# The last down projection of a hybrid encoder block: its sixth feature tile in one pass, and the final norm of the first 256 tokens moved behind it

## The chip, the cores and the metric

The kernel runs on one core of a Trainium2 chip. The metric is the device time of one execution in microseconds (us). TensorE (PE) multiplies, with its weight loads shown apart (PEld); VectorE (DVE), ScalarE (ACT) and GpSimd (POOL) do the elementwise work; SyncE (SP) issues most of the loads and stores, which 16 DMA engines carry out.

## The reference, cut to what matters

The block has three token mixers, a gated merge, and a feed-forward part with a convolution. The change touches only the end of the feed-forward part and the final norm. For 512 tokens, 1024 features and 2816 hidden units:

```
def conv_glu_ffn(h, w_up, w_conv, b_conv, w_down):
    a, u = jnp.split(h @ w_up, 2, axis=-1)
    return (jax.nn.gelu(dwconv3(a, w_conv, b_conv)) * u) @ w_down
...
x = x + conv_glu_ffn(rms_norm(x, ffn_norm_g[l]), ...)
return rms_norm(x, final_norm_g)

def rms_norm(x, g):
    y = x * lax.rsqrt(jnp.mean(x * x, axis=-1, keepdims=True) + EPS)
    return y * g
```

All is float32. Each token's final scale needs the sum of its squares over all 1024 features, so over all eight feature tiles of 128.

## The kernel before

**Products.** Every float32 operand is split into a high and a low part, and each product of tiles is three matmuls into the same accumulator: high x high, high x low, low x high. The helper `mm3` records them, so that nearly all matmuls have the lines L213, L214 and L215. A sum over the 11 tiles of a half of the hidden units (k = 0 to 10) is 33 matmuls.

**The down projection.** The hidden units are done in two halves. In each half the product with `w_down` is made feature tile by feature tile: the weights stand still, the hidden activations of 512 tokens move, and the result has features on partitions and tokens along the row. It is added to the residual stream `x2[f]`, a 128 x 512 tile for each f from 0 to 7, four of them in one buffer. In the last half, tiles 0 to 4 take this way (loop at L1379 to L1393): after each, ScalarE squares the finished tile, GpSimd adds the squares to `acc3` (128 x 512), and ScalarE multiplies the tile by the gain of the final norm.

**The last tiles.** `last_tiles` (L1221) does the rest, in an order that lets the ends of the work overlap:

1. Tiles 5, 6 and 7, the first 256 tokens only (`half_tile`: 33 matmuls of 256 columns, then L1237 adds to the residual, L1239 squares, L1240 adds the squares to `acc3`, L1241 multiplies by the gain). Now `acc3` is complete for the first 256 tokens; `two_parts` (L301, L302) splits it into high and low.
2. Tile 5, the other 256 tokens, again 33 matmuls. Behind its k=5 and k=7 stand the two matmuls of `sum_a` (L1251), which sum `acc3` over the partitions. `rstd_wide` (L337 to L341: two operations on ScalarE, three on VectorE) makes the scale of each token out of that.
3. `out_a(0)` multiplies tiles 0 to 3 of the first 256 tokens by that scale (L1257, four operations on VectorE) and stores them (L1260, to outa, 512 KB).
4. Two blocks of 128 tokens (t=2: tokens 256 to 383; t=3: tokens 384 to 511) finish tiles 6 and 7. Here the activations stand still and the weights of both tiles move (256 columns), so that tokens lie on partitions; again 33 matmuls each. In block t=2, behind k=4, `sums` (L1292, L1294) takes the sums of squares of `acc3` for the tokens of both blocks, GpSimd's power (L1218) and L1311 put one of them where block t=3 will read it, and `out_a(4)` scales and stores tiles 4 to 7 of the first 256 tokens. At the end of block t=2, L1334 evicts it, L1336 squares it, L1337 and a GpSimd power make the scale of its tokens, L1340 puts that on a diagonal, L1342 scales the block and L1343 stores it (outc, 128 KB).
5. In block t=3, behind k=7, `row_b` spreads the scale of tokens 256 to 383 over the partitions with a matmul (L1271), scales tiles 0 to 5 of these tokens (L1274, two operations on VectorE) and stores them (L1276, outc, 384 KB). Then tiles 0 to 5 of the last 128 tokens are transposed (L1288), the sum of squares is finished (L1322), a GpSimd power makes the scale, and the two halves of the last block are stored, one from SP (L1327) and one from ScalarE's queue (L1332), to outb, 256 KB each.

A scheduling layer fixes each engine's order of instructions when the program is built. It follows the source, but may put an operation behind a later one that it takes to be ready sooner. Each engine then works through its list in order, and so does each queue of stores.

Of the kernel before, what the change touches and what calls it, by code (L numbers as in the profile page):

```python
# [18 lines left out]
S = 512  # L19
D = 1024  # L20
KT = D // P
# [5 lines left out]
LF = KT - 2  # L27
# [83 lines left out]
def hybrid_block(ctx, tc, xg, xT, memT, wflat, vecs, gbias, nabias, outa, outb, outc):  # L111
# [14 lines left out]
    def nm(s):  # L126
        uid[0] += 1
        return f"{s}_{uid[0]}"
# [4 lines left out]
    def scr(n=512):  # L133
        return sp.tile([P, S], F32, tag="scr", name=nm("s"))[:, :n]

    def tiny(n):
        return tp.tile([P, 32], F32, tag="tiny", name=nm("y"), bufs=12)[:, :n]

    def mmps():
        return mmp.tile([P, 512], F32, tag="mm", name=nm("mm"))  # L140
# [71 lines left out]
    def mm3(ps, lh, ll, rh, rl, start, stop):  # L212
        PE.matmul(ps, lh, rh, start=start, stop=False)  # L213
        PE.matmul(ps, lh, rl, start=False, stop=False)  # L214
        st["mm"] = PE.matmul(ps, ll, rh, start=False, stop=stop).ins  # L215
# [179 lines left out]
    def proj(key, XHs, XLs, n=S, at={}, ps=None):  # L395

        ws = weights(key)
        k0 = 0 if ps is None else 1
        if ps is None:
            ps = mmps()  # L400
        for k in range(k0, KT):
            mm3(ps[:, :n], ws[k][0], ws[k][1], XHs[k], XLs[k], k == 0, k == KT - 1)
            if k in (1, 3, 5):
                flush()
            if k in at:
                at[k]()
        return ps
# [67 lines left out]
    for f in range(4):  # L475
        ps = ps_k[f] if f < 2 else proj(("mlk", f), XH, XL)
# [27 lines left out]
    for c in range(3):  # L504
        n, nk = TMC[c], TMK[c]
        pss = [(mmps if c % 2 else atps)() for _ in range(NT)]
        for h in range(KT // nk):
            ws = weights(("tm", c, h))
            for t in range(NT):
                tsl = slice(t * P, (t + 1) * P)  # L510
                for k in range(nk):
                    kk = nk * h + k
                    ps = pss[t][:, :n]
                    mm3(ps, XH[kk][:, tsl], XL[kk][:, tsl], ws[k][0], ws[k][1], kk == 0, kk == KT - 1)
        for t in range(NT):
            ps = pss[t]
# [562 lines left out]
    def paced(key):  # L1079
        return proj(key, XH, XL, at={k: lambda: step(RB / 4) for k in (1, 3, 5)})  # L1080

    xq = unit()
    for f in range(4):
        ps = proj(("xaq", f), XH, XL)
# [3 lines left out]
    for f in range(4):  # L1088
        ps = paced(("o", f))
# [15 lines left out]
    for f in range(4):  # L1105
        ps = proj(("memk", f), MH, ML, M)
# [15 lines left out]
    for f in range(4):  # L1122
        ps = paced(("naq", f))
# [3 lines left out]
    for f in range(4):  # L1127
        ps = paced(("nak", f))
# [12 lines left out]
    for br in range(3):  # L1141
# [19 lines left out]
        for fp in range(4):  # L1161
# [9 lines left out]
            for i in range(2):  # L1171
                f = 2 * fp + i
                ps = mmps()
# [22 lines left out]
    for f in range(KT):  # L1196
        xr = scr()
        SY.dma_start(xr, xT[f])
        ps = proj(("out", f), GH, GL)
# [4 lines left out]
        else:  # L1204
            sq = scr()
# [7 lines left out]
    Hf = S // 2  # L1213
    half = {}

    def power(v):
        col = tiny(v.shape[-1])
        G.tensor_tensor(col, v, nhalf[:, :v.shape[-1]], op=ALU.pow)  # L1218
        return col

    def last_tiles(U, UL_):  # L1221

        ws = [w for i in range(3) for w in weights(("dnl", i))]
        w5 = weights(("dn", 1, LF - 1, 0)) + weights(("dn", 1, LF - 1, 1))

        def half_tile(f, cs, at={}):
            ps = mmps()[:, :Hf]
            fs = slice((f - LF) * P, (f - LF + 1) * P) if f >= LF else slice(0, P)  # L1230
            for k in range(HF):
                w = ws[k] if f >= LF else w5[k]
                mm3(ps, w[0][:, fs], w[1][:, fs], U[k][:, cs], UL_[k][:, cs], k == 0, k == HF - 1)
                if k in at:
                    at[k]()
            xf = x2[f][:, cs]
            V.tensor_tensor(xf, ps, xf, op=ALU.add)  # L1237
            sq = scr(Hf)
            A.activation(sq, xf, AF.Square)  # L1239
            V.scalar_tensor_tensor(acc3[:, cs], acc3[:, cs], EPS * D / P if f == KT - 1 else 0.0, sq, op0=ALU.add, op1=ALU.add)  # L1240
            A.activation(xf, xf, AF.Copy, scale=vcol("fin_g", f))  # L1241

        for f in range(LF - 1, KT):
            half_tile(f, slice(0, Hf))

        parts = two_parts(acc3[:, :Hf], Hf)

        def sum_a(i):
            if i == 0:
                half["s"] = atps()  # L1250
            PE.matmul(half["s"][:, :Hf], onesr, parts[i], start=i == 0, stop=i == 1)  # L1251
            if i == 1:
                half["r"] = rstd_wide(half["s"], Hf, None)

        def scale_a(eng, *tiles):
            for i in tiles:
                eng.tensor_tensor(x2[i][:, :Hf], x2[i][:, :Hf], half["r"], op=ALU.mult)  # L1257

        def store_a(i):
            SY.dma_start(outa[i * P:(i + 4) * P, :].rearrange("(f p) s -> p f s", p=P), x2v[i // 4][:, :, :Hf])  # L1260

        half_tile(LF - 1, slice(Hf, S), {5: lambda: sum_a(0), 7: lambda: sum_a(1)})
        def out_a(i):
            scale_a(V, *range(i, i + 4))
            store_a(i)

        out_a(0)
        def row_b():

            pb = atps()  # L1270
            PE.matmul(pb[:, :P], ones, half["e"], start=True, stop=True)  # L1271
            o, tsl = half["o"], slice(2 * P, 3 * P)
            for u, n in ((0, 4), (1, LF - 4)):
                V.tensor_tensor(o[:, u * S:u * S + n * P].rearrange("p (f s) -> p f s", f=n), x2v[u][:, :n, tsl],  # L1274
                                pb[:, :P].unsqueeze(1).to_broadcast([P, n, P]), op=ALU.mult)
            SY.dma_start(outc[:, :LF * P], o[:, :LF * P])  # L1276

        banks = [mmps(), mmps()]
        for t in range(2, NT):
            tsl = slice(t * P, (t + 1) * P)  # L1280
            last = t == NT - 1
            bank = banks[t - 2]
            ps = bank[:, :256]
            pts = [atps() if last else None, mmps()]
            r = scr(256)

            def turn(i):
                PE.transpose(pts[i // 4][:, i % 4 * P:(i % 4 + 1) * P], x2[i][:, tsl], ident)  # L1288

            def sums(sl):  # L1290
                pc = atps()
                PE.matmul(pc[:, :1], acc3[:, sl], ones[:, 0:1], start=True, stop=True)  # L1292
                v0 = tiny(1)
                V.tensor_scalar(v0, pc[:, :1], 1.0 / D, EPS, op0=ALU.mult, op1=ALU.add)  # L1294
                return v0

            for k in range(HF):
                mm3(ps, U[k][:, tsl], UL_[k][:, tsl], ws[k][0], ws[k][1], k == 0, k == HF - 1)
                if k == 1 and last:

                    for i in range(LF, KT):
                        PE.matmul(ps[:, (i - LF) * P:(i - LF + 1) * P], x2[i][:, tsl], ident, start=False, stop=False)
                elif k == 1:
                    for i in range(LF, KT):
                        turn(i)
                    A.activation(r, pts[1][:, 256:], AF.Copy)
                if not last and k == 4:
                    v0 = sums(tsl)

                    v1 = sums(slice(S - P, S))  # L1310
                    V.scalar_tensor_tensor(banks[1][:, 256:257], v1, D ** 0.5, power(v1), op0=ALU.mult, op1=ALU.mult)  # L1311
                    out_a(4)
                if last and k == 7:
                    row_b()
            if last:
                for i in range(LF):
                    turn(i)
            sq, v = scr(257), tiny(1)
            if last:
                oa, ob = scr(), scr()  # L1320

                A.activation(sq, bank[:, :257], AF.Square, scale=D ** -0.5, accum_out=v)  # L1322
                A.activation(oa[:, 256:], pts[0][:, 256:], AF.Copy)
                col = power(v)
                A.activation(oa[:, :256], pts[0][:, :256], AF.Copy, scale=col)
                first = V.tensor_scalar(oa[:, 256:], oa[:, 256:], col, None, op0=ALU.mult).ins
                SY.dma_start(outb[:, :512], oa)  # L1327

                with tc.issue_after(first):
                    V.scalar_tensor_tensor(ob[:, 256:], ps, col, gfin, op0=ALU.mult, op1=ALU.mult)  # L1330
                A.activation(ob[:, :256], pts[1][:, :256], AF.Copy, scale=col)
                A.dma_start(outb[:, 512:], ob)  # L1332
                continue
            V.tensor_tensor(r, ps, r, op=ALU.add)  # L1334
            ss = tiny(1)
            A.activation(sq[:, :256], r, AF.Square, accum_out=ss)  # L1336
            V.tensor_scalar(v, ss, 1.0 / D, v0, op0=ALU.mult, op1=ALU.add)  # L1337
            col = power(v)
            half["e"] = scr(P)
            V.tensor_scalar(half["e"], ident, col, None, op0=ALU.mult)  # L1340
            half["o"] = o = unit()
            V.scalar_tensor_tensor(o[:, LF * P:D], r, col, gfin, op0=ALU.mult, op1=ALU.mult)  # L1342
            SY.dma_start(outc[:, LF * P:], o[:, LF * P:D])  # L1343

    for hh in range(2):
# [3 lines left out]
        for j in range(HF):  # L1349
            f = HF * hh + j  # L1350
            if f == 0:
# [8 lines left out]
                k = KT - 1  # L1360
# [8 lines left out]
            sq = scr()  # L1369
# [9 lines left out]
        for f in range(KT if hh == 0 else LF - 1):  # L1379
            ws = weights(("dn", hh, f, 0)) + weights(("dn", hh, f, 1))  # L1380
            ps = mmps()
# [3 lines left out]
            if hh == 1:  # L1385
# [3 lines left out]
                else:  # L1389
                    sq = scr()  # L1390
# [119 lines left out]
```

## Time and profile before

| | us |
|---|---|
| median of 3 runs | 875.1 (875.02 to 875.71) |
| the profiled execution | 874.76 |
| its span in the profile | 873.0 |
| TensorE busy | 867.6 |
| VectorE busy | 593.4 |
| ScalarE busy | 470.7 |
| GpSimd busy | 125.0 |

The granted TensorE clock was 0.999 of full speed. The span runs from the first to the last event of the program; the rest of the device time lies around it. Times in the views are counted from the start of the span. Line numbers with an L are lines of the kernel that was profiled. A row of the timeline gives start, duration, engine, line, operation, output<-input, and in brackets how long the engine had been idle and what released it. "PE 128*128" is the stationary operand, the next size what moves.

### The profile page before, as it was taken

Reading aid. Unit: us, or ns where it says so; the run is one execution under the profiler, and the core shown is the slowest. Engines: PE = TensorE matmul, PEld = TensorE weight load, DVE = VectorE, ACT = ScalarE, POOL = GpSimd, SP = SyncE. Lnnn points to the kernel's source line nnn. Section 1 sums busy time; section 2 is a strip of 40 time slices with the busy share of each in tenths; the row PEclk is TensorE's granted clock in tenths of the full one; section 3 lists DMA queues with packets and bytes.
Section 4 is the critical chain, followed back from the end, with each engine's and each line's share of the span. In section 5 each row is a group of like instructions: output and inputs, shape, how many; then the busy total and the mean of one; then the engine's idle time right before and its main releaser. Section 6 shows DMA issues by size and latency. Waiting matters only on the chain.

```text
span 873.0 us, 12227 instructions
## 1 busy us (share of the span) xinstructions
PE 867.6 (99%) x4303; PEld 735.9 (84%) x4303; DVE 593.4 (68%) x1240; ACT 470.7 (54%) x996; POOL 125.0 (14%) x201
## 2 busy tenths in 40 slices
PE   9999999999999999999999999999999999999997
PEld 7898889888888888888888888888888888888887
DVE  7794789886577768897676558776633466666534
ACT  7563567765455658898544455444422344444532
POOL 0101100000163370600000002111100011111010
PEclk9999999999999999999999999999999999999999
DMA  8324634522253453633233432332233332322412
GB/s 281 100 79 153 204 122 124 169 82 99 83 143 74 118 151 109 158 121 121 98 97 109 145 108 97 97 97 96 76 100 105 107 98 97 98 96 90 136 40 97
DMA packets 39421, 99.81 MB, mean 114 GB/s; under 512 B 5688, under 2 KB 13880, under 8 KB 39360
## 3 DMA queue, kind: packets, MB, share of 16 engines
q1 hardware_dynamic: 31568, 92.32, 33.3%
q0 software_dynamic: 7360, 6.32, 3.5%
q8 instruction: 34, 0.56, 0.3%
q10 hardware_dynamic: 432, 0.39, 0.1%
q14 instruction: 27, 0.22, 0.1%
HBM read 94.80 MB, written 4.21 MB: 113 GB/s over the span
## 4 chain that ended last, share of the span: by engine, by line
PE 98%; DVE 1%; issue 0%; ACT 0%; POOL 0%; POOLq 0%
PE mm L213 29%; PE mm L214 29%; PE mm L215 29%; PE at L214 2%; PE at L213 2%; PE at L215 2%; PE at L938 1%; PE at L761 1%; PE at L919 1%; PE at L900 0%; PE at L901 0%; PE at L748 0%; PE at L1026 0%; PE at L243 0%; PE mm L422 0%
## 5 line engine op out<-in xcount | busy, mean ns | idle before, releaser
L213 PE MATMUL mm<-u,wh 128*128 128x512 f32 (+1 forms) x1072 | 415.0, 387 | 0.0
L215 PE MATMUL mm<-u,wl 128*128 128x512 f32 (+1 forms) x1072 | 411.8, 384 | 0.0
L214 PE MATMUL mm<-u,wh 128*128 128x512 f32 (+1 forms) x1072 | 411.6, 384 | 0.0
L195 ACT ACTIVATE wh<-wr 128x512 fp32r<-128x512 f32 (+2 forms) x298 | 183.7, 621 | 207.1 <-PE mm L214 163.7
L196 DVE TENSOR_TENSOR wl<-wr,wh 128x512 fp32r<-128x512 f32 (+3 forms) x300 | 203.6, 681 | 89.8 <-ACT wh L195 86.7
L215 PEld LDWEIGHTS mm<-u,wl 128*128 128x128 f32 x1072 | 201.4, 188 | 40.2 <-DVE wl L196 0.2
L213 PEld LDWEIGHTS mm<-u,wh 128*128 128x128 f32 x1072 | 201.5, 188 | 38.6 <-ACT wh L195 0.2
L214 PEld LDWEIGHTS mm<-u,wh 128*128 128x128 f32 x1072 | 201.6, 188 | 38.2
L1374 POOL TENSOR_TENSOR s<-s,rb 128x512 f32<-128x512 f32 x22 | 38.2, 1735 | 402.6 <-DVE s L1373 238.9
L542 POOL DMA_DIRECT2D u<-nav_d x128 | 62.3, 511 | 67.2 <-PE at L938 22.7
L219 ACT ACTIVATE u<-s 128x512 fp32r<-128x512 f32 x26 | 16.4, 632 | 57.9 <-DVE s L1377 56.2
L1377 DVE TENSOR_TENSOR s<-mm,s 128x512 f32<-128x512 f32 x22 | 15.2, 690 | 23.8 <-POOL s L1374 23.8
L462 ACT ACTIVATE s<-pad,vec 128x512 f32<-128x512 f32 x30 | 24.4, 813 | 9.7 <-DVE pad L460 9.7
L220 DVE SCALAR_TENSOR_TENSOR u<-s,u 128x512 fp32r<-128x512 f32 x26 | 19.0, 732 | 14.8 <-ACT u L219 14.7
L463 DVE SCALAR_TENSOR_TENSOR s<-pad,vec,s 128x512 f32<-128x512 f32 x30 | 22.5, 750 | 5.5 <-ACT s L462 5.5
L1373 DVE SCALAR_TENSOR_TENSOR s<-s,s 128x512 f32<-128x512 f32 x22 | 15.2, 691 | 13.4 <-ACT s L1372 13.3
L464 DVE SCALAR_TENSOR_TENSOR s<-pad,vec,s 128x512 f32<-128x512 f32 x30 | 22.5, 750 | 0.8
L1372 ACT ACTIVATE s<-s 128x512 f32<-128x512 f32 x22 | 13.9, 632 | 14.9 <-DVE s L1371 14.9
L460 DVE TENSOR_TENSOR pad<-mm,rb 128x512 f32<-128x512 f32 x22 | 15.1, 690 | 6.5 <-PE mm L215 6.4
L1384 DVE TENSOR_TENSOR u<-mm,u 128x512 f32<-128x512 f32 x13 | 9.0, 691 | 14.6 <-PE mm L215 14.6
L213 PE MATMUL mm<-wh,u 128*128 128x512 f32 x48 | 18.8, 392 | 0.0
L214 PE MATMUL mm<-wl,u 128*128 128x512 f32 x48 | 18.7, 390 | 0.0
(341 smaller groups left out, 1051.5 us busy)
## 6 DMA issues: line engine op xcount, KB each, us to landing
wr<-wflat SPq DMA_DIRECT2D x141, 512.0 KB, 3.4
nab<-nabias SPq DMA_DIRECT2D x16, 256.0 KB, 2.7
u<-nav_d POOLq DMA_DIRECT2D x128, 32.0 KB, 2.8
s<-xT SPq DMA_DIRECT2D x15, 256.0 KB, 4.0
wr<-wflat SPq DMA_DIRECT2D x14, 192.0 KB, 2.4
nav_d<-nv POOLq DMA_DIRECT2D x8, 256.0 KB, 3.7
R<-rd SPq DMA_DIRECT2D x8, 256.0 KB, 5.4
wr<-wflat SPq DMA_DIRECT2D x2, 544.0 KB, 3.4
```

Of the source, the lines that this page charges most:

```text
L195: A.activation(h[:, u:v], src, AF.Copy)
L196: V.tensor_tensor(l[:, u:v], src, h[:, u:v].bitcast(F32), op=ALU.subtract)
L213: PE.matmul(ps, lh, rh, start=start, stop=False)
L214: PE.matmul(ps, lh, rl, start=False, stop=False)
L215: st["mm"] = PE.matmul(ps, ll, rh, start=False, stop=stop).ins
L219: A.activation(h, src, AF.Copy, scale=scale)
L220: V.scalar_tensor_tensor(l, src, scale, h.bitcast(F32), op0=ALU.mult, op1=ALU.subtract)
L462: A.activation(t1, pad[:, 0:512], AF.Identity, scale=vcol(w, i), bias=vcol(b, i))
L463: V.scalar_tensor_tensor(t1, pad[:, 1:513], vcol(w, n + i), t1, op0=ALU.mult, op1=ALU.add)
L464: V.scalar_tensor_tensor(t1, pad[:, 2:514], vcol(w, 2 * n + i), t1, op0=ALU.mult, op1=ALU.add)
L542: G.dma_start(vw[r * 32:(r + 1) * 32, i * 256:(i + 1) * 256], nav_v[hf, r, CW[b]:CW[b] + 32, hp * 256:(hp + 1) * 256])
L1374: G.tensor_tensor(c, c, rb2, op=ALU.mult)
```

## The change

Tile 5 of the last half is multiplied in one pass over all 512 tokens ahead of tiles 6 and 7, in place of two passes over 256. With the second pass gone, what stood beside it moves into the blocks: the matmuls of `sum_a` behind k=5 and k=7 of block t=2, `out_a(0)` behind k=7 of block t=2, and `out_a(4)` from k=4 of block t=2 to k=2 of block t=3. The token sums (`sums`) move from k=4 to k=2 of block t=2.

```diff
-        def half_tile(f, cs, at={}):
-            ps = mmps()[:, :Hf]
+        def part_tile(f, cs):
+            n = cs.stop - cs.start
+            ps = mmps()[:, :n]
...
-                if k in at:
-                    at[k]()
...
-            sq = scr(Hf)
+            sq = scr(n)
...
-        for f in range(LF - 1, KT):
-            half_tile(f, slice(0, Hf))
+        part_tile(LF - 1, slice(0, S))
+        for f in range(LF, KT):
+            part_tile(f, slice(0, Hf))
...
-        half_tile(LF - 1, slice(Hf, S), {5: lambda: sum_a(0), 7: lambda: sum_a(1)})
         def out_a(i):
             scale_a(V, *range(i, i + 4))
             store_a(i)
 
-        out_a(0)
...
-                if not last and k == 4:
+                if not last and k == 2:
                     v0 = sums(tsl)
...
+                if not last and k in (5, 7):
+                    sum_a(k // 6)
+                if not last and k == 7:
+                    out_a(0)
+                if last and k == 2:
                     out_a(4)
```

In the built program this gives the following orders. On VectorE, behind tile 7: the two operations of `sums` (L1292 after the change), the write for block t=3 (L1309), then L302, L339, the eviction of block t=2 (L1337), L340, L341, the four scalings of `out_a(0)`, the tiny operation of the scale of tokens 256 to 383 (L1340), one scaling of `out_a(4)`, the diagonal (L1343), L1345, the other three scalings, and the two operations of `row_b` (L1272). On TensorE, the matmul of `row_b` (L1269) stands two matmuls later than before, in k=8 of block t=3. On SP, the store of block t=2 (L1346) goes ahead of the second outa store, and the large outc store (L1274) and the first outb store (L1330) behind it.

## The prediction

> **What bounds the kernel now.** I read the page first, then busy time by stage, then the last 31 us engine by engine, and last the DMA.
>
> ```profile
> span 873.0 us, 12227 instructions
> PE 867.6 (99%) x4303; PEld 735.9 (84%) x4303; DVE 593.4 (68%) x1240; ACT 470.7 (54%) x996; POOL 125.0 (14%) x201
> PE 98%; DVE 1%; issue 0%; ACT 0%; POOL 0%; POOLq 0%
> ```
>
> TensorE is busy through the whole span and carries 98% of the chain that ended last. So a gain or a loss is either TensorE time, or time behind the last matmul, where stores end the span. The change touches only the last 31 us. Next, busy time by stage (length; busy time of PE, PEld, DVE, ACT, POOL; granted clock; DMA share; GB/s). The stages are feature tile 4 at 512 tokens, the first half of tile 5, the halves of tiles 6 and 7, the second half of tile 5 with two row-sum matmuls in it, block t=2, block t=3.
>
> ```profile
> 834.82:842.29 7.47, 7.47 (x34) 6.19 (x33) 2.63 (x4) 2.93 (x5) 1.29 (x1) 1.00 0.15 59
> 842.29:846.25 3.96, 3.96 (x35) 3.95 (x33) 0.69 (x1) 1.36 (x2) 1.29 (x1) 1.00 0.00 0
> 846.25:854.02 7.77, 7.77 (x69) 7.77 (x67) 1.70 (x4) 1.86 (x4) 0.00 (x0) 1.00 0.01 2
> 854.02:858.26 4.24, 4.24 (x37) 4.24 (x36) 1.29 (x4) 2.15 (x5) 0.00 (x0) 1.00 0.00 0
> 858.26:862.92 4.66, 4.66 (x41) 4.62 (x40) 4.16 (x15) 1.13 (x3) 0.69 (x1) 1.00 0.11 34
> 862.92:867.51 4.59, 4.59 (x41) 4.59 (x40) 2.74 (x8) 0.51 (x2) 0.56 (x1) 1.00 0.68 226
> ```
>
> TensorE has no gap and runs at full clock, so these lengths are its prices. VectorE is nearly full in block t=2 (4.16 of 4.66 us) and loosely filled before it (1.29 of 4.24). The stores of the first 256 tokens are most of the DMA share of block t=3. TensorE's marks in the tail:
>
> ```profile
> 857.06 0.28 PE L1251 MATMUL at<-s,onesr 128*128 128x256 f32 x1
> 860.28 0.58 PE L1292 MATMUL at<-ones,acc 128*128 128x1 f32 x4
> 861.75 0.28 PE L215 MATMUL mm<-u,u 128*128 128x256 f32 x1
> 866.23 0.38 PE L1271 MATMUL at<-s,ones 128*128 128x128 f32 x2
> 867.39 0.28 PE L215 MATMUL mm<-u,u 128*128 128x256 f32 x1
> ```
>
> The row at 861.75 is the last matmul of k=7 in block t=2, the one at 867.39 the last of the 33 of block t=3. The other engines in the same stretch:
>
> ```profile
> 857.38 0.38 ACT L337 ACTIVATE s<-at 128x256 f32<-128x256 f32 x1 [1.31 <-PE at L1251]
> 858.25 0.43 DVE L339 SCALAR_TENSOR_TENSOR s<-at,s 128x256 f32<-128x256 f32 x1 [1.72 <-ACT s L338]
> 859.37 0.43 DVE L341 SCALAR_TENSOR_TENSOR s<-s,s 128x256 f32<-128x256 f32 x1
> 860.05 1.42 DVE L1257 TENSOR_TENSOR u<-u,s 128x256 f32<-128x256 f32 x4
> 861.39 0.21 DVE L1294 TENSOR_SCALAR y<-at 128x1 f32<-128x1 f32 x2
> 861.68 0.69 POOL L1218 TENSOR_TENSOR y<-y,nhalf 128x1 f32<-128x1 f32 x1 [16.39 <-DVE y L1294]
> 862.40 0.17 DVE L1311 SCALAR_TENSOR_TENSOR mm<-y,y 128x1 f32<-128x1 f32 x1 [0.47 <-POOL y L1218]
> 862.48 1.09 DVE L1257 TENSOR_TENSOR u<-u,s 128x256 f32<-128x256 f32 x3
> 864.48 0.21 DVE L1337 TENSOR_SCALAR y<-y,y 128x1 f32<-128x1 f32 x1 [0.58 <-ACT s L1336]
> 864.77 0.56 POOL L1218 TENSOR_TENSOR y<-y,nhalf 128x1 f32<-128x1 f32 x1 [2.40 <-DVE y L1337]
> 865.36 0.29 DVE L1340 TENSOR_SCALAR s<-ident,y 128x128 f32<-128x128 f32 x1 [0.67 <-POOL y L1218]
> 865.57 0.48 DVE L1342 SCALAR_TENSOR_TENSOR u<-s,y,gbf 128x256 f32<-128x256 f32 x1
> 867.71 0.39 ACT L1322 ACTIVATE s<-mm 128x257 f32<-128x257 f32 x1 [3.27 <-PE mm L215]
> ```
>
> Then the stores: when the queues issue them, and the DMA while they move.
>
> ```profile
> 861.54 2.49 SPq L1260 DMA_DIRECT2D outa<-u  x2
> 866.07 0.34 SPq L1343 DMA_DIRECT2D outc<-u  x1
> 867.69 0.34 SPq L1276 DMA_DIRECT2D outc<-u  x1
> 869.35 0.33 SPq L1327 DMA_DIRECT2D outb<-s  x1
> 869.72 0.35 ACTq L1332 DMA_DIRECT2D outb<-s  x1
> ```
>
> ```profile
> 862.25:862.50 0.25, 0.25 (x5) 0.25 (x4) 0.10 (x2) 0.00 (x0) 0.12 (x1) 1.00 0.09 29
> 862.25:864.25 2.00, 2.00 (x20) 2.00 (x19) 1.50 (x5) 0.32 (x1) 0.12 (x1) 1.00 0.77 256
> 868.50:869.75 1.25, 0.00 (x0) 0.00 (x0) 0.74 (x2) 0.87 (x3) 0.31 (x1) 1.00 0.81 315
> 870.00:871.75 1.75, 0.00 (x0) 0.00 (x0) 0.00 (x0) 0.00 (x0) 0.00 (x0) 0.64 0.81 300
> 871.50:871.75 0.25, 0.00 (x0) 0.00 (x0) 0.00 (x0) 0.00 (x0) 0.00 (x0) 0.50 0.27 90
> ```
>
> Share times length is the time for which all 16 DMA engines are full: 0.77 x 2.00 = 1.54 us for the first outa store, 0.81 x 1.25 = 1.01 us for the large outc store, 0.81 x 1.75 = 1.42 us for the two outb stores together. Today these three groups do not meet. The last data move until 871.50 + 0.27 x 0.25 = 871.57, and the span ends 873.0 - 871.57 = 1.43 us later.
>
> **TensorE's part.** Tile 5 is now one pass of 33 matmuls over 512 tokens. Tile 4 shows its price, 7.47 us; removed are two passes of 3.96. The second pass lasted 4.24, and the 0.28 above 3.96 are the two row-sum matmuls, which only move. The saving is 2 x 3.96 - 7.47 = 0.45 us. Per matmul that is 0.226 us at 512 tokens and 0.120 at 256.
>
> The Trainium skill (TensorE: Matmul & The Clock Gate, Back-to-back issue gap) gives a warm gap of 262 cycles at 256 columns and 518 at 512, at 2.4 GHz 0.109 and 0.216 us, by which the pass would save only 66 x 0.109 - 33 x 0.216 = 0.07 us and everything below would come 0.38 us later. The trace differs in both gaps, and I keep its rows.
>
> Block t=2 therefore begins at 842.29 + 7.47 + 7.77 = 857.53 (now 858.26). It takes 4.66 + 0.28 = 4.94 us, since the row-sum matmuls lie in it, and block t=3 begins at 862.47 (now 862.92).
>
> **The norm of the first 256 tokens.** The built order puts the second row-sum matmul behind k=7, which is 861.75 + 0.12 - 858.26 = 3.61 us into the block, plus 0.16 for the first one: 861.30. It needs the low part, L302, which VectorE now runs behind L1292 and L1309 (L1294 and L1311 before), so behind a GpSimd power. The token sums move from k=4 to k=2, six matmuls or 0.72 us earlier in the block: 857.53 + 2.02 - 0.72 = 858.83, and end 0.58 later at 859.41. From L1294 to L1311 it takes 862.40 - 861.39 = 1.01, to the next VectorE operation 0.08 more; L302 (0.43, as L339) ends at about 860.93. TensorE does not wait, with 0.37 us to spare.
>
> From the second row-sum matmul ScalarE's first operation is 857.38 - 857.06 = 0.32 us away, L339 1.19 us: 862.49. Now the eviction of block t=2 stands between L339 and L340, where an eviction stood before too, so L341 follows 859.37 - 858.25 = 1.12 us later, at 863.61, and the first scaling at 864.04, when L341 ends. Four scalings take VectorE 861.39 - 860.05 = 1.34 us. Here the order costs something: the tiny operation that starts the norm of tokens 256 to 383 (L1340 after, L1337 before) is queued behind them and runs at 865.38 instead of 864.48, 0.90 us later, though its input is there by then. Behind it, a fifth scaling runs beside the GpSimd power, which I price at the 0.69 us of the row beside wide VectorE work and not at 0.56. So the scaled identity comes 0.90 + 0.13 later, at 866.39, ends at 866.68, and L1345 (L1342 before) starts at 866.60.
>
> TensorE wants that scaled identity (L1269) in k=8 of block t=3, two matmuls later than now: 862.47 + (866.23 - 862.92) + 0.24 = 866.02. It waits 0.66 us there, with all later matmuls and the transposes behind it. The last matmul is then 866.68 + (867.39 - 866.23) - 0.24 = 867.60 (now 867.39), and the tail of block t=3 starts 0.21 us later: the 0.45 is gone.
>
> **The stores.** L1345 holds VectorE for about 0.40 us before the next operation starts (its rows overlap by some 0.08), then three scalings take 1.09: 867.00 + 1.09 = 868.09. The second outa store follows 0.07 later (861.54 against 860.05 + 1.42), at 868.16. Before, both outa stores were issued by 864.03 (861.54 + 2.49). On SP's queue the large outc store and the first outb store come behind it, and none waits long to be issued: the large outc store needs two VectorE operations more, the outb stores come at about 869.6 and 869.9. The data of an outa store start 862.50 - 0.09 x 0.25 - 861.54 = 0.94 us after the issue, so at 869.10. From there the 16 engines have 1.54 + 1.01 + 1.42 = 3.97 us of work without a gap, because each following store is issued before the one ahead has drained. Data end at 873.07, the span 1.43 later at 874.50, against 873.0: +1.50 us. The 0.45 us is inside this number; the tail that it meets is 1.95 us worse.
>
> The bounds of the terms: the GpSimd power at 0.56 takes 0.13 off; the outc store's 384 KB in 1.01 us is 389 GB/s, and the whole backlog (512 + 384 + 512 KB) at that rate takes 3.70, 0.27 off; the outa store's own rate (512 KB in 1.54, 340 GB/s) for all of it takes 4.24, 0.27 on.
>
> The Trainium skill (DMA: Bandwidth & Descriptors, Where 436 GB/s comes from) puts the ceiling at 435 GB/s, by which the backlog would take an estimated 3.31 us and the end would come 0.66 us sooner. The stores of this trace stay below that rate.
>
> The profiled execution is 874.76 us for a span of 873.0, and 0.34 below the median of 875.1. Added to that median: **876.6 us**. This kernel's runs tell about 0.2%, 1.75 us, from no change.
>
> **Rivals.** First, *the stores stay hidden*: SP issues the second outa store so early, or the engines drain so fast, that the last outb store ends the span as now. Then only the 0.21 us of TensorE's late end is left: 875.3; if the scaled identity also came in time, 874.65. For it speaks that the engines stand idle for 0.6 us ahead of the outb data now (868.50 + 1.01 = 869.51 to 871.57 - 1.42 = 870.15), against it that the issue of the second outa store hangs on VectorE's order, which is built in. It would need that store to be issued by 873.0 + 0.21 - 1.43 - 3.97 - 0.94 = 866.87.
>
> Second, *one DMA engine lags*. The two outa stores landed differently:
>
> ```profile
> DMA to landing us min/median/max: 3.0/3.3/3.7
> ```
>
> A store lands when its slowest engine is done, and one took 0.7 us longer than its twin. Now such a lag is hidden in block t=3. With an outa store at the head of the last backlog a late engine carries its delay through to the last outb store: 876.6 + 0.7 = 877.3, slower beyond the bound from a lag of 0.25 us. Against it: with the backlog, other engines' idle time does not help, but the lag may as well have come from the second store queuing behind the first, which the backlog already contains.
>
> Third, *the saving shows*: 875.1 - 0.45 = 874.65, if neither VectorE's order nor the stores cost anything. It is 0.05%, so even this is no change by the bound.
>
> **How the numbers follow.** The forecast, a store backlog that ends between 875.8 and 877.1 by the bounds above, gets 0.68. The hidden stores (with the saving) get 0.11, the lagging engine 0.19, anything better by over 0.2%, which no row supports, 0.02. 876.85 is the bound to slower: the upper sixth of the forecast, about 0.12, lies above it. So slower 0.31, within 0.2% 0.67, faster 0.02. The range 875.3 to 877.3 reaches down to the hidden stores and up to the lagging engine.
>
> **What would show it.** Tile 5 as 33 matmuls in about 7.5 us, and block t=3 starting 0.4 to 0.5 us earlier. The tiny operation L1340 starting right behind four scalings, and TensorE waiting 0.5 to 0.8 us at L1269. The second outa store issued at about 868.2, and the DMA share full without a gap from about 869 to 873. I am wrong if the DMA has a gap there, if the second outa store is issued before 867, or if TensorE waits at the second row-sum matmul instead.

## The result, and the profile after

| | before | after |
|---|---|---|
| median of 22 runs, us | 875.18 (874.66 to 875.89) | 876.63 (876.09 to 877.21) |
| ratio | | 1.0016, 95% interval 1.0009 to 1.0023 |
| span of the profiled execution, us | 873.0 | 875.4 |

The change costs 1.45 us (by the interval 0.8 to 2.0). It is slower beyond the noise of 22 runs, and smaller than the 0.2% that the prediction took as its bound.

The two spans differ by more, and part of that is not the change. In the profiled execution of the changed kernel the first matmul of tile 5 starts at 843.34, and not at 842.29, though nothing ahead of it was changed in the source. The profiles of e1 to e7 below show the same kind of shift, with starts from 842.67 to 843.39. So I count times from the start of tile 5. A page rounds the span to 0.1 us; to two digits the traces have 872.95 before and 875.44 now. The span ends 872.95 - 842.29 = 30.66 us after the start of tile 5 before the change, and 875.44 - 843.34 = 32.10 after it now, which is 1.44 us more and agrees with the runs.

The page of the changed kernel, and busy time by stage (tile 5; tiles 6 and 7; block t=2; block t=3):

```profile
span 875.4 us, 12160 instructions
PE 868.3 (99%) x4270; PEld 735.4 (84%) x4270; DVE 593.9 (68%) x1238; ACT 470.5 (54%) x994; POOL 124.9 (14%) x201
```

```profile
843.34:850.82 7.48, 7.48 (x35) 6.20 (x33) 0.69 (x1) 1.35 (x2) 1.29 (x1) 1.00 0.01 2
850.82:858.59 7.77, 7.77 (x67) 7.77 (x66) 2.23 (x4) 2.29 (x4) 0.00 (x0) 1.00 0.00 0
858.59:863.40 4.81, 4.81 (x43) 4.81 (x42) 1.66 (x6) 2.40 (x6) 0.57 (x1) 1.00 0.00 0
863.40:868.87 5.47, 4.86 (x41) 4.65 (x40) 4.89 (x15) 0.54 (x3) 0.67 (x1) 1.00 0.27 90
```

Tile 5 takes 7.48 us in one pass, against 3.96 twice. Block t=3 starts 863.40 - 843.34 = 20.06 us after tile 5, against 862.92 - 842.29 = 20.63: 0.57 us saved up to there. VectorE's full stretch has moved from block t=2 (now 1.66 of 4.81 us) to block t=3 (4.89 of 5.47), and block t=3 has a hole of 5.47 - 4.86 = 0.61 us on TensorE. The timeline shows what stands around the hole:

```profile
862.21 0.28 PE L1251 MATMUL at<-s,onesr 128*128 128x256 f32 x1
867.72 0.49 PE L1269 MATMUL at<-s,ones 128*128 128x128 f32 x2 [0.61 <-DVE s L1343]
868.75 0.28 PE L215 MATMUL mm<-u,u 128*128 128x256 f32 x1
```

```profile
865.04 1.43 DVE L1257 TENSOR_TENSOR u<-u,s 128x256 f32<-128x256 f32 x4
866.39 0.21 DVE L1340 TENSOR_SCALAR y<-y,y 128x1 f32<-128x1 f32 x1
866.51 0.41 DVE L1257 TENSOR_TENSOR u<-u,s 128x256 f32<-128x256 f32 x1
866.67 0.67 POOL L1218 TENSOR_TENSOR y<-y,nhalf 128x1 f32<-128x1 f32 x1 [5.45 <-DVE y L1340]
867.38 0.29 DVE L1343 TENSOR_SCALAR s<-ident,y 128x128 f32<-128x128 f32 x1 [0.45 <-POOL y L1218]
867.98 1.09 DVE L1257 TENSOR_TENSOR u<-u,s 128x256 f32<-128x256 f32 x3
```

The tiny operation L1340 starts right behind the four scalings, the GpSimd power runs beside a fifth, and the diagonal L1343 is what TensorE waits for at L1269. The last three scalings hold back the second outa store. The queues, the landing times in the list of DMA issues (KB, median us to landing), and the DMA share in the last stretch:

```profile
866.54 0.39 SPq L1260 DMA_DIRECT2D outa<-u  x1
868.09 0.34 SPq L1346 DMA_DIRECT2D outc<-u  x1
869.14 0.38 SPq L1260 DMA_DIRECT2D outa<-u  x1
870.02 0.33 SPq L1274 DMA_DIRECT2D outc<-u  x1
870.71 0.36 SPq L1330 DMA_DIRECT2D outb<-s  x1
871.08 0.35 ACTq L1335 DMA_DIRECT2D outb<-s  x1
```

```profile
outb<-s SPq DMA_DIRECT2D x1, 256.0 KB, 3.5
outb<-s ACTq DMA_DIRECT2D x1, 256.0 KB, 3.4
```

```profile
870.00:874.25 4.25, 0.00 (x0) 0.00 (x0) 0.75 (x2) 0.84 (x2) 0.17 (x1) 0.92 0.94 339
874.00:874.25 0.25, 0.00 (x0) 0.00 (x0) 0.00 (x0) 0.00 (x0) 0.00 (x0) 0.50 0.06 17
```

From 870.0 on the engines are full for 0.94 x 4.25 = 4.00 us without a gap. The last matmul starts at 868.75, and the span ends 6.65 us later. An outb store lands 3.4 to 3.5 us after its issue. Before the change, with the engines idle ahead of the outb data, the same two stores took 2.0 and 2.3:

```profile
outb<-s SPq DMA_DIRECT2D x1, 256.0 KB, 2.0
outb<-s ACTq DMA_DIRECT2D x1, 256.0 KB, 2.3
```

### The profile page after: what moved, and what is told of

Its sections match the earlier page's. It is cut to its first block, busy times and chain, and to the rows that moved or that the text cites. A ratio compares the mean times of both kernels' runs of the same rounds, so it can differ in the third digit from the quotient of the medians.

```text
span 875.4 us, 12160 instructions
## 1 busy us (share of the span) xinstructions
PE 868.3 (99%) x4270; PEld 735.4 (84%) x4270; DVE 593.9 (68%) x1238; ACT 470.5 (54%) x994; POOL 124.9 (14%) x201
## 4 chain that ended last, share of the span: by engine, by line
PE 98%; DVE 0%; issue 0%; ACT 0%; POOL 0%; POOLq 0%; ACTq 0%
PE mm L213 29%; PE mm L215 29%; PE mm L214 29%; PE at L214 2%; PE at L215 2%; PE at L213 2%; PE at L938 1%; PE at L761 1%; PE at L919 1%; PE at L900 0%; PE at L901 0%; PE at L748 0%; PE at L1026 0%; PE at L243 0%; PE mm L422 0%
## 5 line engine op out<-in xcount | busy, mean ns | idle before, releaser
L215 PEld LDWEIGHTS mm<-u,wl 128*128 128x128 f32 x1061 | 199.4, 188 | 40.5
L462 ACT ACTIVATE s<-pad,vec 128x512 f32<-128x512 f32 x30 | 24.4, 813 | 9.7 <-DVE pad L460 9.7
L213 PE MATMUL mm<-wh,u 128*128 128x512 f32 x48 | 18.8, 393 | 0.0
L215 PE MATMUL mm<-wh,u 128*128 128x512 f32 x48 | 18.7, 390 | 0.0
```

The lines of the kernel that those rows point to most:

```text
L462: A.activation(t1, pad[:, 0:512], AF.Identity, scale=vcol(w, i), bias=vcol(b, i))
```

## The experiments

Theory A is the prediction's: the second outa store is issued late and leads a backlog that ends the span; TensorE's wait has no part in that sum, and the merged pass does save its time. Theory B says that TensorE's wait and its late last matmul end the span. Theory C says that the merged pass saves nothing where it stands. The changed kernel and the kernel before it have 22 runs each; each experiment has 11, beside 33 (e1 to e4) or 27 (e5 to e7) of the kernel before on the same chip. "From tile 5" is the end of the span counted from the first matmul of tile 5 (both from the trace, in the column before it), less the 30.66 us of before.

| | median, us | before, us | ratio (95%) | span less start of tile 5, us | from tile 5, us |
|---|---|---|---|---|---|
| changed kernel | 876.63 | 875.18 | 1.0016 (1.0009 to 1.0023) | 875.44 - 843.34 | +1.44 |
| e1 early store | 875.82 | 875.34 | 1.0006 (0.9997 to 1.0015) | 874.05 - 843.06 | +0.33 |
| e2 no TensorE wait | 876.79 | 875.34 | 1.0018 (1.0009 to 1.0026) | 875.49 - 843.39 | +1.44 |
| e3 norm first | 876.87 | 875.34 | 1.0018 (1.0010 to 1.0027) | 874.97 - 842.72 | +1.59 |
| e4 late store alone | 876.68 | 875.34 | 1.0017 (1.0008 to 1.0026) | 874.78 - 842.71 | +1.41 |
| e5 saving alone | 874.90 | 875.37 | 0.9994 (0.9985 to 1.0003) | 872.78 - 842.67 | -0.55 |
| e6 two passes | 877.07 | 875.37 | 1.0021 (1.0012 to 1.0030) | 875.64 - 843.17 | +1.81 |
| e7 store a bit late | 875.78 | 875.37 | 1.0005 (0.9996 to 1.0014) | 873.90 - 842.79 | +0.45 |

By the intervals of the runs alone, the rival theory's time is excluded in e2 (only just), e3 and e4. In e1, e5, e6 and e7 it lies inside the interval, and the profile decides.

**e1: the second outa store early, TensorE's wait left in.**

```diff
+                if not last and k == 3:
+                    store_a(4)
                 if not last and k == 7:
                     out_a(0)
-                if last and k == 2:
-                    out_a(4)
```

> The changed kernel, but tiles 4 to 7 of the first 256 tokens are left unscaled, so that their store (the second outa store) needs no scale and goes out in block t=2, ahead of the first. Matmuls, TensorE's wait at L1269 and the four other scalings stay. Theory A (the late second outa store leads a backlog of stores that ends the span): the backlog begins with the large outc store instead, its 1.54 us at the DMA engines are gone from it, and the last outb store, issued at its present time, ends the span: about 1.0 us less than the changed kernel, 875.6. Theory B (TensorE's wait of 0.61 us and the late last matmul end the span, the stores are hidden): nothing that B counts has changed, 876.6.

Measured: 875.82, and +0.33 from tile 5, 1.11 less than the changed kernel, where A expected about 1.0 and B nothing. The wait is still there, and the backlog is broken; the DMA share has a gap ahead of the outb data:

```profile
867.33 0.49 PE L1269 MATMUL at<-s,ones 128*128 128x128 f32 x2 [0.62 <-DVE s L1343]
868.49 0.28 PE L215 MATMUL mm<-u,u 128*128 128x256 f32 x1
869.75:871.00 1.25, 0.00 (x0) 0.00 (x0) 0.75 (x2) 0.84 (x2) 0.15 (x1) 1.00 0.80 312
871.00:871.25 0.25, 0.00 (x0) 0.00 (x0) 0.00 (x0) 0.00 (x0) 0.00 (x0) 1.00 0.00 0
871.25:873.00 1.75, 0.00 (x0) 0.00 (x0) 0.00 (x0) 0.00 (x0) 0.00 (x0) 0.76 0.81 300
```

With the store away, what is left over the kernel before is TensorE's late end: the last matmul starts 868.49 - 843.06 = 25.43 us after the start of tile 5 against 867.39 - 842.29 = 25.10 before, which is 0.33 us too. The prediction had put it at 0.21.

**e2: TensorE's wait taken away, the stores left as they are.**

```diff
-                if last and k == 7:
+                if last and k == 9:
                     row_b()
```

> The changed kernel with the matmul of row_b behind k=9 of block t=3 instead of k=7. The scaled identity is then there when TensorE comes to it. Theory A: TensorE's wait goes (0.61 us to under 0.1), the last matmul and the issue of the outb stores come 0.5 to 0.6 us sooner, and the end does not move, because the second outa store is issued as before and the engines stay full from then on: 876.6, within 0.15. Theory B: 0.5 to 0.6 us less, 876.0 to 876.1.

Measured: 876.79, and +1.44 from tile 5, the same as the changed kernel, so A. L1269 has no wait any more, the last matmul starts 24.94 us after the start of tile 5 and not 25.41, the second outa store is issued at 25.80 as in the changed kernel, and the engines are as full as ever, 0.89 x 4.50 = 4.00 us of work.

```profile
867.77 0.49 PE L1269 MATMUL at<-s,ones 128*128 128x128 f32 x2
868.33 0.28 PE L215 MATMUL mm<-u,u 128*128 128x256 f32 x1
870.50 0.62 SPq L1330 DMA_DIRECT2D outb<-s  x1
870.79 0.35 ACTq L1335 DMA_DIRECT2D outb<-s  x1
870.00:874.50 4.50, 0.00 (x0) 0.00 (x0) 0.70 (x3) 0.63 (x2) 0.00 (x0) 0.91 0.89 320
```

The outb stores are issued only 0.26 and 0.34 us sooner (27.11 and 27.40 after the start of tile 5, in place of 27.37 and 27.74), less than the 0.5 to 0.6 that I had expected. A wait of 0.6 us on TensorE, which carried 98% of the chain before, was worth nothing while the stores were the last to finish.

**e3: VectorE's order changed, the norm of tokens 256 to 383 ahead of most scalings.**

```diff
-                if not last and k == 7:
-                    out_a(0)
...
             SY.dma_start(outc[:, LF * P:], o[:, LF * P:D])
+            out_a(0)
```

> The changed kernel with out_a(0) behind the norm of tokens 256 to 383 in the source: VectorE then runs one scaling, the tiny operation of that norm, one scaling, the diagonal, the scaled block, and then the other six scalings. The diagonal is ready about 0.8 us sooner, so TensorE does not wait; the first outa store goes out about 1.3 us later, the second at the same time as now. Theory A: the backlog now begins with the first outa store, about 867.8 by the clock of the profile before, and has 2 x 1.54 + 1.01 + 1.42 us: the end moves by 0 to +0.3, 876.6 to 876.9. Theory B: TensorE's 0.6 us come back, 876.0.

Measured: 876.87 and +1.59 from tile 5, 0.15 more than the changed kernel and inside A's 0 to 0.3; the runs alone cannot tell 0.15 from nothing. TensorE does not wait, and both outa stores now stand at the head of the backlog, 0.94 x 6.00 = 5.64 us of it:

```profile
866.10 0.49 PE L1269 MATMUL at<-s,ones 128*128 128x128 f32 x2
867.75:873.75 6.00, 0.56 (x6) 0.32 (x3) 2.29 (x7) 1.60 (x5) 0.61 (x1) 0.77 0.94 328
```

**e4: the kernel before, with nothing but a late second outa store.**

```diff
...
-                    out_a(4)
                 if last and k == 7:
                     row_b()
+                    with tc.issue_after(half["b"]):
+                        out_a(4)
```

(`half["b"]` is the second VectorE operation of `row_b`, named in a part that is not shown; what stands in `tc.issue_after` is put behind it.)

> The kernel before (tile 5 in two passes, no wait on TensorE), changed in one thing: the four scalings of tiles 4 to 7 of the first 256 tokens stand behind the two operations of row_b, so that the second outa store is issued at about 869.1 instead of 863.6. Theory A: data from 870.0, 1.54 + 1.42 us of work ahead of the end, 1.4 us more than before: 876.5. Theory B: TensorE is as before; VectorE's last two operations come up to 0.1 us later: 875.1 to 875.3.

Measured: 876.68, +1.41 from tile 5. Tile 5 is still in two passes and TensorE still has no wait, and yet nearly the whole loss of the changed kernel is there:

```profile
866.64 0.38 PE L1271 MATMUL at<-s,ones 128*128 128x128 f32 x2
868.11 0.33 SPq L1276 DMA_DIRECT2D outc<-u  x1
869.50 0.38 SPq L1260 DMA_DIRECT2D outa<-u  x1
870.25:873.50 3.25, 0.00 (x0) 0.00 (x0) 0.02 (x1) 0.12 (x1) 0.00 (x0) 1.00 0.92 323
```

The large outc store is issued 868.11 - 842.71 = 25.40 us after the start of tile 5, as before (867.69 - 842.29 = 25.40), so its delay in the changed kernel (26.68) is not needed for the loss. VectorE's last two operations came 0.26 us later than before, and not up to 0.1; that too is far from 1.41. The loss comes out so near that of the changed kernel because the store is 0.99 us later here (26.79 against 25.80), with 1.01 us less work behind it.

**e5: the merged pass without the late stores.**

```diff
-                if not last and k == 7:
-                    out_a(0)
-                if last and k == 2:
-                    out_a(4)
+                if not last and k in (1, 3):
+                    store_a(2 * k - 2)
```

> The changed kernel without the eight scalings of the first 256 tokens: both outa stores go out unscaled, early in block t=2; the row sums and the rest of that norm are still worked out, and not used. Theory A (the merged pass does save 0.45 us of TensorE time, and only the late stores and VectorE's queue take it back): no wait at L1269, no backlog, the end 0.4 to 0.5 us ahead of the kernel before: 874.8 to 874.9 beside 875.34. Theory C (the merged pass saves nothing where it stands, the stage just shifts): as before, 875.3.

Measured: 874.90, 0.47 below the kernel before, at the edge of what 11 runs can tell (the interval just includes 1); from tile 5 it is 0.55, and the last matmul starts 867.21 - 842.67 = 24.54 us after the start of tile 5, 0.56 sooner than before. One thing is not as expected: the built order put the first outa store at 838.9, ahead of tile 5, and only the second, at 859.6, in block t=2. The stages show the saving without a hole behind it:

```profile
842.67:850.15 7.48, 7.48 (x35) 6.20 (x33) 0.69 (x1) 1.35 (x2) 1.29 (x1) 1.00 0.01 2
857.92:862.73 4.81, 4.81 (x43) 4.81 (x42) 1.66 (x6) 2.40 (x6) 0.57 (x1) 1.00 0.32 109
862.73:867.33 4.60, 4.60 (x41) 4.60 (x40) 3.19 (x9) 0.54 (x3) 0.56 (x1) 1.00 0.10 32
867.21 0.28 PE L215 MATMUL mm<-u,u 128*128 128x256 f32 x1
```

So theory C falls.

**e6: the changed kernel with two passes again.**

```diff
-        part_tile(LF - 1, slice(0, S))
+        part_tile(LF - 1, slice(0, Hf))
+        part_tile(LF - 1, slice(Hf, S))
```

> The changed kernel with tile 5 in two passes of 256 tokens again, both ahead of tiles 6 and 7; everything else as changed. Theory A: block t=2 and all behind it, the stores too, come 0.45 us later: 1.8 us more than before, 877.1. Theory C: as the changed kernel, 876.7.

Measured: 877.07. By the runs alone this is 0.4 above the changed kernel, within their intervals. From tile 5 it is +1.81, which is 0.37 more than the changed kernel where A had 0.45, and the second outa store is 0.38 later (26.18 against 25.80). The profile has the price itself, 7.93 for the two passes against 7.48 for one:

```profile
843.17:851.10 7.93, 7.93 (x68) 7.93 (x67) 1.54 (x3) 2.29 (x4) 1.29 (x1) 1.00 0.01 2
```

**e7: the kernel before, its second outa store a little late.**

```diff
-                    out_a(4)
...
+            with tc.issue_after(done):
+                out_a(4)
```

(behind the first store to outc at the end of block t=2; `done` is the scaled block.)

> The kernel before, changed in one thing: the four scalings of tiles 4 to 7 of the first 256 tokens stand behind the scaled block of tokens 256 to 383 (L1342 of before), so that the second outa store is issued at about 867.1, between 863.6 (before) and 868.2 (changed). Theory A, by the prediction's sum: data from 868.05, then 1.54 + 1.01 + 1.42 us without a gap and 1.43 to the end of the span, 873.45 against 873.0: 0.45 us more than before, 875.8. Theory B (only TensorE and what follows its last matmul count): as before, 875.3.

Measured: 875.78, +0.45 from tile 5, as the sum gave. That is a little too good: the store is issued 867.70 - 842.79 = 24.91 us after the start of tile 5, where the sum had 867.1 - 842.29 = 24.81, and with the issue as measured the same sum gives 0.54. It is 26.79 in e4 and 25.80 in the changed kernel; in the kernel before the store was issued by 864.03, 21.74 after the start of tile 5.

```profile
867.70 0.38 SPq L1260 DMA_DIRECT2D outa<-u  x1
868.50:872.75 4.25, 0.36 (x4) 0.12 (x2) 0.80 (x3) 1.40 (x5) 0.55 (x1) 0.88 0.94 339
```

A version that beats both kernels did not follow. The saving is about 0.05%. In the changed kernel the span ends 32.10 - 25.80 = 6.30 us after the issue of the second outa store, so by an estimate from that the store would have to be issued by 24.4 us after the start of tile 5 for an end no later than before (30.66), and by 23.8 for the whole saving of e5 (30.11). The norm of the first 256 tokens cannot begin before tile 7 ends, which the merged pass puts 3.5 us later (858.59 - 843.34 = 15.25 against 854.02 - 842.29 = 11.73). Whether another order on VectorE or GpSimd's help could make that up was not tried.

## Why the prediction was right, point by point

All in us; the first two rows and the work of the engines are lengths, the others are times from the start of tile 5:

| step | predicted | measured |
|---|---|---|
| tile 5 in one pass | 7.47 | 7.48 |
| block t=2 | 4.94 | 4.81 |
| second row-sum matmul | 19.01 | 18.87 |
| first scaling | 21.75 | 21.70 |
| L1340, behind four scalings | 23.09 | 23.05 |
| diagonal L1343 | 24.10 | 24.04 |
| L1269 on TensorE | 24.39 | 24.38 |
| last matmul | 25.31 | 25.41 |
| second outa store issued | 25.87 | 25.80 |
| work of the engines from there | 3.97 | 4.00 |
| last data | 30.78 | 30.67 |
| end of the span | 32.21 | 32.10 |

**The saving** of the merged pass was right (0.45; e6 shows 7.93 against 7.48) and is real (e5). It is worth 0.12 us more up to block t=3 (0.57), because block t=2 is shorter than I took it to be: I moved the two row-sum matmuls at the full price that they had beside tile 5, and the token sums at 0.58, where their row now says 0.50.

```profile
859.88 0.50 PE L1290 MATMUL at<-ones,acc 128*128 128x1 f32 x4
```

Which wait of before was in those rows the runs do not show.

**TensorE's wait** came at the place that VectorE's order gave, and L1269 started within 0.01 us of the sum. The 0.61 us of the profile is not the count of the prediction's 0.66: the profile counts idle time behind the whole of the matmul before, the prediction from the time at which TensorE would have started L1269. That time is 863.40 + 3.31 + 0.24 = 866.95 now, so by the prediction's count the wait is 867.72 - 866.95 = 0.77, longer because block t=3 began earlier. e2 shows that it costs nothing while the stores are late. e1 shows that it would cost something otherwise, 0.33 us where the prediction had 0.21. The sum took 1.16 - 0.24 = 0.92 us from L1269 to the last matmul, and it took 868.75 - 867.72 = 1.03. In the changed kernel this error does not reach the end.

**The stores** were the right term. e1 takes the backlog away, and what is left is TensorE's late end; e4 puts only the late store into the kernel before and gets +1.41, where the changed kernel has +1.44; e7 puts it in between and gets +0.45. The price of 3.97 us for the last four stores held to 0.03, since it came from the same stores with the same rows.

**Two other prices.** By an estimate from the gaps in the Trainium skill (TensorE: Matmul & The Clock Gate, Back-to-back issue gap) the merged pass would have been nearly worthless, 0.07 us. Tile 5 in the changed kernel and in e6 has 0.45 for it. By an estimate from the ceiling of 435 GB/s in the Trainium skill (DMA: Bandwidth & Descriptors, Where 436 GB/s comes from) the backlog would have been 0.66 us shorter. The trace has 4.00 us for it against the sum's 3.97, so the rows were the better price in both places.

**The rivals.** The hidden stores were excluded by VectorE's order, as argued: the rival needed the second outa store by 866.87 - 842.29 = 24.58 us after the start of tile 5, and it was issued at 25.80. The lagging engine did not come: in the changed kernel the two outa stores land alike, in 2.9 to 3.0 us, where before they took 3.0 and 3.7.

```profile
DMA to landing us min/median/max: 2.9/2.9/3.0
```

**What was luck.** The forecast was 876.6 and the median is 876.63; the sum said +1.50, and the runs moved by 1.45 and the profile by 1.44. That the numbers meet so closely is partly luck, since errors cancelled. The sum ends at 32.21, 0.11 later than the measured 32.10, but it set this against a span that the page had rounded up by 0.05, and it was added to a median of 3 runs that lay 0.08 below that of 22. Inside the sum, the short block t=2 brought the second row-sum matmul 0.14 us ahead of the sum, but ScalarE and VectorE took 0.09 us longer from there to the first scaling, so that the scaling was only 0.05 early and the store 0.07. The interval of the runs, 1.2 us wide, cannot tell such differences apart. The spread of 875.8 to 877.1 that the prediction gives for its backlog is also wider than the bounds that it names, which come to 876.2 to 876.9; what the rest stands for it does not say, and the chance of 0.12 above 876.85 rests on it.

## What to carry to other kernels

A stage that looks like slack, here a second pass that costs 0.45 us, may be the cover that lets a norm and a megabyte of stores drain before the end: before taking it out, count when the last large store can be issued and how many microseconds of transfers are queued behind it. At the end of a kernel, count bytes from that issue on. In these runs the DMA engines had no gap from there to the last store, and a wait on TensorE that did not delay that issue was free (e2); what moved the end was the time of that issue (e1, and e7 against e4). A delay that reaches that issue is not free: in e6 the store went out 0.38 us later and the end came 0.37 later.

## What the runs showed of the hardware that I had not expected

Profiles of kernels with the same source up to tile 5 reach it at times up to 1.10 us apart (842.29 before, 843.39 in e2), nearly as large as the effect under study. Counted from the start of tile 5, single profiles agreed with each other far more closely: the changed kernel and e2 both end at 32.10, e1's end and its last matmul are both 0.33 late, and block t=2 lasts 4.81 in the changed kernel and in e5. Eleven runs with an interval of 0.18%, or 1.6 us, could not show differences of this size. No kernel was profiled twice here, so the spread of two profiles of one kernel from tile 5 on is not shown.
